# The first layer's down product in two groups of three token tiles, the contexts in the first

## The chip, the cores and the metric

The kernel runs on one core of a Trainium2 chip. The metric is the device time of one execution in microseconds (us). Three timed runs of the kernel before gave 1691.24, 1693.2 and 1694.03 us, a median of 1693.2.

The engines are named as the profile names them: PE (TensorE, matrix products; PEld is its weight load), DVE (VectorE), ACT (ScalarE), POOL (GpSimd) and SP (SyncE, which here issues nearly all transfers).

## The reference

Two layers over 512 latent tokens with a prefix of 256 context tokens, model width 1024. Layer 0 mixes tokens by attention, layer 1 by a state-space recurrence (S5). Each is followed by a gated convolutional feed-forward net of inner width 2816. What lies around the change is the end of layer 0 and the mixer of layer 1:

```
# end of layer 0, for the latents and, with their own m, for the contexts
x  = x + m[5] * rms_norm(conv_ffn(h), g_post_ffn)       # conv_ffn ends with  (silu(gate)*val) @ w_down
# layer 1
u  = modulate(rms_norm(x, g_pre_mix), m[0], m[1])       # 64 groups of 16 channels
for d in (forward, backward):
    bu  = einsum('blgc,gnc->blgn', u, bb[d])            # complex, 64 states a group
    h_c = scan(lb[d], bu of the contexts)               # h[t] = lb*h[t-1] + bu[t]
    h_l = scan(lb[d], bu of the latents, start = last h_c)
    y_l = y_l + readout(h_l, c[d])
o  = (gelu(y_l + d*u) @ w_glu_a) * sigmoid(gelu(...) @ w_glu_b)
```

Of the contexts layer 1 needs the end states of the scan alone: they are where the scan of the latents starts.

## The kernel before

Tokens lie in tiles of 128 rows: two of contexts (tiles 0 and 1, `range(NTC)`) and four of latents (`range(NTC, NT)`). Products in fp32 are made of three matmuls on operands split into a high and a low part (`mm3`, lines 145 to 147). A weight comes from memory as a raw tile of 512 KB over SP's queue, ACT makes its high part (L108) and DVE its low part (L109); five raw tiles and four split ones are kept.

**The down product** (`ffn0`, `ffn_down`) has two groups, each with its own pass over the 22 weight tiles of `w_down`: first the four latent tiles, then the two context tiles. An accumulator `dn` of one token tile has 1024 columns of PSUM; three such stand in one place (`big`), the fourth tile's in another. When a tile's sum is done, `post_start` squares it on ACT (L721), multiplies it by its gate row on DVE into a buffer `po` (L722, two buffers in turn) and makes its norm (L164 to L170). L727 adds the stream `px`; then come the statistics of layer 1's norm, its scale on POOL (L1007) and its shift on DVE (L1008). The result in `po` is sent (L1013) to `xc` (latents) or `xcc` (contexts), where tokens are laid out for the recurrence in steps of eight. A `po` buffer is free again when its transfer has landed. The rows of gates, scales and shifts (`rows`, 512 KB each, L982) are loaded for each group in its pool.

**The recurrence.** `ssm_turn` lays tokens out by channel: a copy (L1362), PE transposes `pu` (L1367), copies to `u` (L1370, L1372). `ssm_inputs` makes the inputs in units: products `pi` with a constant matrix `Pt` (512 KB, L1401), a copy `pe` (L1405), transposes `pb` (L1387) and two copies to `B` (L1392). A unit is 2 of 32 channel pairs for the latents (16 units), and 4 for the contexts (8 units, states in `Bc`). `ssm_spans` runs the recurrence inside spans of eight steps, in seven steps `k`: POOL multiplies (L1425), DVE multiplies (L1428) and adds (L1429, L1431). Latents have four blocks of channels, and so 4 x 7 steps; contexts two halves, 2 x 7. `ssm_carry` (L1440 to L1443, four DVE instructions) takes a state from span to span: three carries for a half of the contexts (`first`), seven for a pair of latent blocks (`local`). `states` then puts the carries into all steps of a block (L1562 to L1565), 8 copies `SA` for each block (L1572) set them for the readout `py` (L1586 to L1588), and ACT's GELU, transposes `pg` (L1607) and the split `gT` (L1612, L1613) feed the GLU product `glu`.

**What sets the order.** The framework orders each engine's instructions by a timeline of its own; in ties and waits it goes by the order in which the code emits them. Under the second group's loop the code takes steps of a generator `ssm_latents`, so the latents' turns and the first half of their input units are emitted between the context tiles' matmuls; the contexts' own turn, inputs, spans and carries follow in `ssm`. Buffers come from pools that are opened and closed in order: a pool opened where another was closed uses its memory, and its first writer waits for the last user there.

Of the kernel before, what the change touches and what calls it, by code (L numbers as in the profile page):

```python
# [19 lines left out]
P = 128  # L20
# [111 lines left out]
class Kernel:  # L132
# [693 lines left out]
    def ffn_up(self, l, acts, side, jobs, njobs, mods, before=None):  # L826
# [5 lines left out]
        self.hps = [self.pool(f"h{l}{i}", side) for i in range(len(acts))][::-1]  # L832
# [67 lines left out]
    def ffn_down(self, tiles, i, nhs, done, hold=False, jobs=None, ends=3, last=False):  # L900

        W, nc, ps = self.W, self.nc, self.ps
        half, h = NF // 2, self.h[i]
        pool, pn = self.hsp, h[0].shape[2]
        cols = range(0, pn, P)
        acc = [ps.tile([P, D], FT, name="dn", tag="big", bufs=3) for _ in tiles[len(tiles) // 4:]]
# [5 lines left out]
        def parts(f):  # L912
            for i in range(f, min(f + 3, NF)):
                if i not in ss:
                    s = pool.tile([P, 2, pn], FR, name="hs", tag="hs", bufs=nhs)
                    x = h[i // half][:, i % half]
# [10 lines left out]
        def together(fs, each):  # L927
            ws = [W.take(ahead=min(3, NF - f) if hold else 3) for f in fs]
            for f in fs:
                parts(f)  # L930
            for i in range(len(tiles)):
                for f, w in zip(fs, ws):
                    down(i, f, ss[f], w)
                    if i == len(tiles) - 1:
                        W.done()
                each(i)

        together(range(3), lambda i: None)
        for f in range(3, NF - ends):
# [4 lines left out]
            if jobs:  # L944
                for _ in range(17 * (f - 2) // 15 - 17 * (f - 3) // 15):
                    next(jobs, None)
        together(range(NF - ends, NF), lambda i: done(tiles[i], acc[i]))

    def ffn0(self):
# [41 lines left out]
        xcc = None  # L991
        begun = []

        def begin(t, acc, wk, rows):
            begun.append((t, self.post_start(t, acc, [rows[0], rows[0]], src, wk, 2, 2)))
# [3 lines left out]
        def end(wk, rows):  # L999
# [5 lines left out]
            _, sh, gs = rows  # L1005
# [3 lines left out]
            dst, i, parts = (xc, t - NTC, 2) if t >= NTC else (xcc, t, 4)  # L1009
            n, c = P // TC, D // parts  # L1010
            for a in range(parts):
                p0 = P // parts * a + n * i
                nc.sync.dma_start(dst[p0:p0 + n], o[:, a * c:(a + 1) * c])  # L1013

        def group(i, tiles, hold, jobs, ends, nhs):
            wk = self.pool(f"wkE{i}", "left" if i else "right")
            rows = rows_of(wk, i)
# [6 lines left out]
            self.ffn_down(tiles, i, nhs, done, hold, jobs, ends)  # L1024
            wk.release()
            self.hsp.release()
            if i == 0:
                self.wkD.release()
            self.hps[i].release()

        group(0, range(NTC, NT), False, None, 4, 5)
        sb1 = self.pool("ssmB1", "right")
        self.sb = [sb0, sb1]
        self.hsp = self.pool("hsc")
        self.W.fence = self.glu0
        self.W.limit = self.glu0 + 4
        lats = self.ssm_latents(xc)
        next(lats)
        xcc = self.xcc
        group(1, range(NTC), True, lats, 4, 4)  # L1040
        for _ in lats:
            pass
# [407 lines left out]
    def ssm_latents(self, xc):  # L1450

        nc, sb1 = self.nc, self.sb[1]
        su = self.su = self.pool("ssmu", "right")
        self.banks = (("aux", 2),)
        self.lam_tile(su.tile([P, 2048], FT, name="lam"))
        u = self.u = su.tile([P, G, NCL], FT, name="u")
        uv = u.rearrange("p (a g) j -> p g a j", a=2)
        self.xp = self.pool("ssmp", "right")
        self.xcc = self.xp.tile([4 * NCC, TC, D // 4], FT, name="xcc")
        sx = self.pool("ssmx", "right")  # L1460
        mats = self.ssm_ahead([(self.Pd, gp, 2) for gp in range(0, G // 4, 2)], ((sx, "Pt", 3),))
        next(mats)
        xqs = sb1.tile([P, 4, 8, TC, GC], FT, name="xq", tag="B", bufs=1)
        yield
        for b in range(4):
            yield from self.ssm_turn(xc[:, :, b * P:(b + 1) * P], xqs[:, b], uv[:, 8 * b:8 * b + 8], (nc.scalar, nc.scalar))
        B = self.B = [x.tile([P, 2, NCL + 1, 2, 2, 8], FT, name="B", tag="B", bufs=1) for x in self.sb]
        spans = self.spans = [self.ssm_spans(su, B[b // 2][:, b % 2:b % 2 + 1, 1:], b) for b in range(4)]
        self.us = lambda b: B[b // 2][:, b % 2, 1:], lambda g: u[:, g], NCL
        for gp in self.ssm_inputs(mats, *self.us, sx, 1, (0, G // 4)):  # L1470
            for b in range((gp + 2) // 8):
                if next(spans[b], self) is not self:
                    break
            yield
        sx.release()

    def ssm_contexts(self, mats, sc, si):

        nc, v = self.nc, self.nc.vector
        xq = si.tile([P, 16, TC, GC], FT, name="xqc")  # L1480
        uc = si.tile([P, 16, 4, NCC], FT, name="uc")
        for _ in self.ssm_turn(self.xcc, xq, uc, (v, nc.scalar, v, nc.scalar)):
            pass
        Bc = self.Bc = [sc.tile([P, 2, NCC, 2, 2, 8], FT, name=f"Bc{i}") for i in range(2)]
        self.cspans = [self.ssm_spans(sc, Bc[i], 2 * i) for i in range(2)]
        for gp in self.ssm_inputs(mats, lambda b: Bc[b // 2][:, b % 2], lambda g: uc[:, g % 16, g // 16], NCC, si, 1):
            yield gp

    def ssm(self):
        tc, nc, v = self.tc, self.nc, self.nc.vector  # L1490
        ps, W, u = self.ps, self.W, self.u
        lamR, lamI = self.lam
        sc = self.pool("ssmc")
        si = self.pool("ssmi")
        mats = self.ssm_ahead([(self.Pd, gp, 2) for gp in range(0, G // 2, 2)], ((self.wp, "raw", 5),))
        next(mats)
        W.behind, W.fence = (self.mark,), None
        W.ensure(self.glu0 + 4)
        tiles = []

        def get(ks):
            for k in ks:
                while len(tiles) <= k:
                    tiles.append(next(mats))
                yield tiles[k]

        lats = self.ssm_inputs(get(range(8, 16)), *self.us, si, 1, (G // 4, G // 2))
        self.banks = (("big", 3),)
        for gp in self.ssm_contexts(get(range(16)), sc, si):
            if gp >= 16:  # L1510
                self.banks = (("aux", 2),)
                for _ in range(2):
                    next(lats, None)
                self.banks = (("big", 3),)
        self.banks = (("aux", 2),)
        for _ in lats:
            pass
        si.release()
        self.xp.release()
        sp = self.pool("ssms")  # L1520
# [3 lines left out]
        self.banks = (("aux", 2), ("aux", 2), ("big", 3))  # L1524
        B = self.B
# [3 lines left out]
        def first(i):  # L1529

            spans = [*self.spans[2 * i:2 * i + 2], self.cspans[i]]
            while spans:
                for x in list(spans):
                    if next(x, self) is self:
                        spans.remove(x)
            x = self.Bc[i][:, :, 7]
            for s_ in range(8, NCC, 8):
                last = s_ == NCC - 8
# [255 lines left out]
```

## Time and profile before

| | kernel before |
|---|---|
| timed runs | 1691.24, 1693.2, 1694.03 us |
| profiled execution | 1692.19 us, of which the span of the trace is 1690.4 us |
| mean granted TensorE clock | 0.957 |
| PE busy | 1543.8 us (91%) |
| DVE busy | 1060.1 us (63%) |
| ACT busy | 745.8 us (44%) |
| POOL busy | 169.8 us (10%) |
| DMA | 256.03 MB, mean 151 GB/s |

The span runs from the first to the last recorded instruction, and the execution's time is 1.8 us longer. Shares are averages over the whole span; what a stage costs is read in the rows of that stage. PE's share is high in all but one long stretch, between the end of the down product and the GLU product of layer 1. Times in rows count from the span's start.

### The profile page before, as it was taken

To read this page: it belongs to the slowest core of one execution; us is meant where nothing else is said; L and a number is where in the kernel's file an instruction comes from. 1 tells how busy PE (TensorE), PEld (TensorE's weight loads), DVE (VectorE), ACT (ScalarE), POOL (GpSimd) and SP (SyncE) were. 2 spreads that over 40 slices of the span, in tenths; PEclk is the share of its full clock that TensorE was granted. 3 is DMA by queue.
4 is the path that set the end of the run, shared out by engine and by line. 5 is a ranking of instruction groups with operands and counts; after the bars stand their busy time and mean duration, and the time that the engine had idled before them with its cause. 6 is when DMAs were issued, how large, how long until landed. Compare 5 with 4: busy or idle time off the path is not lost.

```text
span 1690.4 us, 23335 instructions
## 1 busy us (share of the span) xinstructions
PE 1543.8 (91%) x8724; PEld 1228.7 (73%) x8724; DVE 1060.1 (63%) x2052; ACT 745.8 (44%) x1438; POOL 169.8 (10%) x170
## 2 busy tenths in 40 slices
PE   5999689999999999999999987725899999999997
PEld 2776469888888887778788875414678887778886
DVE  4554577768767777867643586699446655455334
ACT  4465457756434332323332356525645433333322
POOL 0111240000000000000000113366011000000000
PEclk7999799999999999999999998876899999999999
DMA  9424460087445656775853596643453234433421
GB/s 306 143 74 130 159 217 26 26 263 244 140 120 166 204 153 189 189 201 159 221 179 100 165 290 210 178 141 103 147 156 120 88 112 125 126 99 113 149 75 50
DMA packets 219847, 256.03 MB, mean 151 GB/s; under 512 B 20318, under 2 KB 171782, under 8 KB 219094
## 3 DMA queue, kind: packets, MB, share of 16 engines
q1 hardware_dynamic: 219302, 254.46, 49.2%
q8 instruction: 69, 1.13, 0.3%
q14 instruction: 44, 0.36, 0.1%
q0 software_dynamic: 384, 0.07, 0.0%
q10 hardware_dynamic: 48, 0.01, 0.0%
HBM read 216.55 MB, written 34.80 MB: 149 GB/s over the span
## 4 chain that ended last, share of the span: by engine, by line
PE 75%; DVE 11%; DMA 6%; ACT 4%; issue 2%; SPq 1%; POOL 0%; DVEq 0%; ACTq 0%; POOLq 0%
PE up L145 12%; PE up L147 11%; PE up L146 11%; PE dn L145 5%; PE dn L146 5%; PE dn L147 5%; PE acc L145 2%; PE acc L147 2%; PE acc L146 2%; PE glu L145 2%; PE glu L147 2%; PE glu L146 2%; PE macc L287 2%; DMA wm<-in_w_mod 1%; DVE t L1428 1%
## 5 line engine op out<-in xcount | busy, mean ns | idle before, releaser
L109 DVE TENSOR_TENSOR whl<-wraw,whl 128x1024 fp32r<-128x1024 f32 x202 | 250.2, 1243 | 210.9 <-ACT whl L108 207.5
L108 ACT ACTIVATE whl<-wraw 128x1024 fp32r<-128x1024 f32 x206 | 217.0, 1056 | 240.6 <-PE dn L147 141.8
L145 PE MATMUL up<-b,whl 128*128 128x256 f32 (+1 forms) x728 | 243.4, 337 | 2.6 <-DVE h L857 2.5
L147 PE MATMUL up<-b,whl 128*128 128x256 f32 (+1 forms) x728 | 241.4, 335 | 0.5 <-DVE whl L109 0.5
L146 PE MATMUL up<-b,whl 128*128 128x256 f32 (+1 forms) x728 | 241.6, 334 | 0.0
L146 PE MATMUL dn<-whl,hs 128*128 128x512 f32 x440 | 172.5, 394 | 5.0 <-DVE whl L109 5.0
L147 PE MATMUL dn<-whl,hs 128*128 128x512 f32 x440 | 171.7, 393 | 0.0
L145 PE MATMUL dn<-whl,hs 128*128 128x512 f32 x440 | 171.4, 394 | 0.0
L145 PEld LDWEIGHTS up<-b,whl 128*128 128x128 f32 x728 | 136.9, 189 | 26.4 <-issue 6.1
L146 PEld LDWEIGHTS up<-b,whl 128*128 128x128 f32 x728 | 137.3, 189 | 16.3 <-issue 2.0
L147 PEld LDWEIGHTS up<-b,whl 128*128 128x128 f32 x728 | 136.4, 189 | 16.5 <-issue 2.2
L146 PE MATMUL up<-c,whl 128*128 128x512 f32 (+1 forms) x384 | 142.6, 373 | 0.1
L147 PE MATMUL up<-c,whl 128*128 128x512 f32 (+1 forms) x384 | 141.9, 372 | 0.0
L145 PE MATMUL up<-c,whl 128*128 128x512 f32 (+1 forms) x384 | 140.8, 375 | 1.1 <-DVE c L338 1.1
L857 DVE SCALAR_TENSOR_TENSOR ga<-up,cw,ga 128x511 f32<-128x511 f32 (+1 forms) x132 | 86.8, 658 | 84.5 <-ACT ga L853 83.1
L853 ACT ACTIVATE ga<-up,cw 128x512 f32<-128x512 f32 x66 | 46.5, 705 | 151.5 <-PE up L147 149.8
L857 DVE SCALAR_TENSOR_TENSOR h<-up,cw,h 128x511 f32<-128x511 f32 (+1 forms) x132 | 86.7, 657 | 37.0 <-ACT h L853 35.9
L146 PEld LDWEIGHTS dn<-whl,hs 128*128 128x128 f32 x440 | 83.1, 189 | 24.5 <-DVE whl L109 6.7
L145 PEld LDWEIGHTS dn<-whl,hs 128*128 128x128 f32 x440 | 83.0, 189 | 18.6 <-ACT ga L853 0.4
L147 PEld LDWEIGHTS dn<-whl,hs 128*128 128x128 f32 x440 | 83.2, 189 | 18.1
L145 PEld LDWEIGHTS up<-c,whl 128*128 128x128 f32 x384 | 71.3, 188 | 18.0 <-issue 4.5
L147 PEld LDWEIGHTS up<-c,whl 128*128 128x128 f32 x384 | 72.3, 188 | 13.4 <-issue 0.4
(352 smaller groups left out, 3009.3 us busy)
## 6 DMA issues: line engine op xcount, KB each, us to landing
wraw<-in_w_up SPq DMA_DIRECT2D x88, 512.0 KB
wraw<-in_w_mod SPq DMA_DIRECT2D x80, 512.0 KB
wraw<-in_w_down SPq DMA_DIRECT2D x66, 512.0 KB
wraw<-in_w_o SPq DMA_DIRECT2D x24, 512.0 KB
Pt<-Pd SPq DMA_DIRECT2D x24, 512.0 KB
Pt<-Qd SPq DMA_DIRECT2D x32, 384.0 KB
wm<-in_w_mod SPq DMA_DIRECT2D x16, 512.0 KB
Pd<-Pb SPq DMA_DIRECT2D x16, 512.0 KB
```

What stands on the lines that cost most here:

```text
L108: nc.scalar.activation(w[:, 0], r, AF.Copy)
L109: e.tensor_tensor(w[:, 1], r, w[:, 0], op=OP.subtract)
L145: nc.tensor.matmul(out, a[0], b[0], start=start, stop=False)
L146: nc.tensor.matmul(out, a[0], b[1], start=False, stop=False)
L147: nc.tensor.matmul(out, a[1], b[0], start=False, stop=stop)
L287: nc.tensor.matmul(acc[32 * q:32 * q + 32], self.cT[:, k, :], w[:, 256 * q:256 * q + 256], start=(k == 0), stop=(k == KD - 1))
L853: nc.scalar.activation(o, acc, AF.Identity, scale=c[:, 1:2], bias=c[:, 3:4])
L857: nc.vector.scalar_tensor_tensor(x, acc[:, a + s:b + s], c[:, tap:tap + 1], x, op0=OP.mult, op1=OP.add)
L1428: v.tensor_tensor(t1, L[:, :, :, k - 1], lr[:, :, None].to_broadcast(shape), op=OP.mult)
```

## The change

The two groups of the down product become groups of three tiles. The first has both contexts and the first latent tile, the second the other three latent tiles. `ffn_down` takes `pieces`, which say from which of the two inner activations each tile's columns come. There are two sets of `rows` in the first group (latent and context), and a new one (`rows_10024` below) for the second.

The contexts no longer go straight to `xcc`: they are written to a buffer in device memory (`xnd`, L1019) and read back into `xcc` (L1486). The generator that runs under the second group's loop is now `ssm_contexts`: the contexts' turn, inputs, spans and carries, 30 steps spread over the loop's passes 6 to 17, which end with the states `C0` from which the latents start. Ahead of the last four passes a function `before` takes what is left of the generator, opens the pool of the second group's posts (`wkE1`) where the contexts' pools were, loads its rows and opens the pool of the latents' `Pt`. The latents' turns, all 16 of their input units, spans and carries are emitted behind the second group, in `ssm`. The contexts' `Pt` tiles and the latents' are loaded apart (16 + 16 loads in place of 24). The first weights of the GLU may be loaded only after the latents' inputs have been emitted (`W.limit`). The last tile's `xc` goes over ACT's queue.

In the order that comes of it, the first group's three tiles have their posts as before. Of the contexts' work, 16 `pu`, 50 of 64 `pi` and 24 of 32 `pb` matmuls stand among the second group's down matmuls, and 14 `pi` and 8 `pb` behind the last of them; the latents' 32 `pu` follow these. The fourth of the contexts' eight units has its `pb` 67 down matmuls ahead of the last one.

```diff
-        self.hps = [self.pool(f"h{l}{i}", side) for i in range(len(acts))][::-1]
+        self.hps = [self.pool(f"h{l}{i}", side) for i in range(len(acts))]
...
-    def ffn_down(self, tiles, i, nhs, done, hold=False, jobs=None, ends=3, last=False):
+    def ffn_down(self, tiles, pieces, nhs, done, jobs=None, ends=3, last=False, before=None):
...
-                    nc.scalar.activation(s[:, 0], x, AF.Copy)
-                    nc.vector.tensor_tensor(s[:, 1], x, s[:, 0], op=OP.subtract)
+                    for j, lo, hi in pieces:
+                        x, c = self.h[j][i // half][:, i % half, lo:hi], slice(o, o + hi - lo)
+                        nc.scalar.activation(s[:, 0, c], x, AF.Copy)
+                        nc.vector.tensor_tensor(s[:, 1, c], x, s[:, 0, c], op=OP.subtract)
...
-                for _ in range(17 * (f - 2) // 15 - 17 * (f - 3) // 15):
-                    next(jobs, None)
+                n, a, z = jobs[0], 6, NF - ends
+                for _ in range(n * (max(f + 1, a) - a) // (z - a) - n * (max(f, a) - a) // (z - a)):
+                    next(jobs[1], None)
+        if before:
+            before()
...
+            if t < NTC:
+                nc.sync.dma_start(self.xnd[t * P:(t + 1) * P, :], o)
+                return
+            n, c, q = P // TC, D // 2, nc.scalar if t == NT - 1 else nc.sync
...
+        wk = self.pool("wkE0", "right")
+        rows = [rows_of(wk, i) for i in range(2)]
+        tiles = range(NTC + 1)
+        self.ffn_down(tiles, ((1, 0, CTX), (0, 0, P)), 5, done_of(wk, rows, tiles), ends=4)
...
+        self.W.fence = self.W.limit = self.glu0
+        jobs = self.ssm_contexts()
...
+        def before():
+            for _ in jobs:
+                pass
+            rest["wk"] = wk = self.pool("wkE1")
+            rest["rows"] = [rows_of(wk, 0), None]
+            self.sx = self.pool("ssmx", "right")
+            self.mats = self.ssm_ahead([(self.Pd, gp, 2) for gp in range(0, G // 2, 2)],
+                                       ((self.wp, "raw", 5), (self.sx, "Pt", 3)))
+            next(self.mats)
...
+        self.ffn_down(tiles, ((0, P, LAT),), 4, done, jobs=(30, jobs), ends=4, before=before)
...
+    def ssm_contexts(self):
...
+        for a in range(4):
+            nc.sync.dma_start(xcc[NCC * a:NCC * a + NCC],
+                              dap(self.xnd, a * (D // 4), [[TC * D, NCC], [D, TC], [1, D // 4]]))
...
+        mats = self.ssm_ahead([(self.Pd, gp, 2) for gp in range(0, G // 2, 2)], ((si, "Pt", 3),))
...
+        def half(i):
+            yield from self.ssm_spans(su, Bc[i], 2 * i)
...
+                o = self.C0[:, i] if last else sc.tile([P, 2, 2, 2, 8], FT, name="cc", tag="cc", bufs=3)
+                self.ssm_carry(su, i, o, x, Bc[i][:, :, s_ + 7])
...
+        first = half(0)
+        for gp in self.ssm_inputs(mats, lambda b: Bc[b // 2][:, b % 2], lambda g: uc[:, g % 16, g // 16], NCC, si, 1):
+            if gp >= 12:
+                next(first, None)
+                next(first, None)
+            yield
+        for _ in first:
+            yield
+        yield from half(1)
+        si.release()
+        sc.release()
...
     def ssm(self):
...
+        for b in range(4):
+            for _ in self.ssm_turn(self.xc[:, :, b * P:(b + 1) * P], xq[:, b], uv[:, 8 * b:8 * b + 8],
+                                   (nc.scalar, nc.vector)):
+                pass
...
+        for gp in self.ssm_inputs(self.mats, lambda b: B[b // 2][:, b % 2, 1:], lambda g: u[:, g], NCL, self.sx, 1):
...
+        W.behind, W.fence, W.limit = (self.mark,), None, self.glu0 + 4
```

DVE at the end of the second group, before: splits of activations and weights, the gate product of the first context tile (`po`, L722), and among them copies of the latents' turn (`u`).

```order
L918 TENSOR_TENSOR hs<-h_4326,hs 128x256
L109 TENSOR_TENSOR whl_9929<-wraw_9767,whl_9929 128x1024
L918 TENSOR_TENSOR hs<-h_4326,hs 128x256
L1370 COPY u<-pu 128x4x2x64
L722 TENSOR_TENSOR po<-dn,rows_9327 128x512
L1370 COPY u<-pu 128x4x2x64
L722 TENSOR_TENSOR po<-dn,rows_9327 128x512
L723 TENSOR_TENSOR sp<-sp 128x1
```

The same place after: `cc`, `cw` and `C` belong to the contexts' carries, `Bc` to their states, and L722 is the gate product of the second group's first tile.

```order
L1466 TENSOR_TENSOR cw<-cc,lam 128x64
L1467 TENSOR_TENSOR cw<-cc,lam 128x64
L1468 TENSOR_TENSOR cw<-cw,Bc_9488 128x64
L1469 TENSOR_TENSOR C_9388<-cw 128x64
L722 TENSOR_TENSOR po<-dn,rows_10024 128x512 x2
L723 TENSOR_TENSOR sp<-sp 128x1
L722 TENSOR_TENSOR po<-dn,rows_10024 128x512
```

Between the last split of the second group's activations and its first L722, DVE now has all 66 instructions of the contexts' spans and carries (14 steps of three, six carries of four); before, these stood behind the posts of the second group.

SP before, where the second group's rows are loaded: between two early weight tiles of that group.

```order
L811 DMA wraw_9053<-in_w_down 128x1024
L982 DMA rows_9327<-md_3544 128x1024
L982 DMA rows_9327<-md_5424 128x1024 x2
L714 DMA px<-xd_3585 128x1024 x2
L811 DMA wraw_9058<-in_w_down 128x1024
```

SP after, from the last weight tile of the second group on; `Qd` holds the readout's matrices.

```order
L811 DMA wraw_9907<-in_w_down 128x1024
L1375 DMA Pt<-Pd 128x1024 x13
L1375 DMA Pt<-Qd 128x768 x8
L1375 DMA Pt<-Pd 128x1024 x6
L991 DMA rows_10024<-md_3544 128x1024
L991 DMA rows_10024<-md_5424 128x1024 x2
L714 DMA px<-xd_3585 128x1024 x2
```

The rows' load moved from the group's start behind its last weight and behind `Pt` loads. Its memory was that of `Bc`, and its wait is on the last instruction that reads `Bc`: L1468 above, three lines ahead of the L722 that needs the rows.

## Rows read from the trace of the kernel before

**Rows 1.** Windows by stage: busy of PE, PEld, DVE, ACT, POOL; clock; DMA share, GB/s.

```profile
961.00:1041.50 80.50, 72.70 (x326) 58.30 (x326) 57.65 (x91) 45.37 (x80) 11.63 (x5) 0.98 0.81 240
1041.50:1168.60 127.10, 60.96 (x465) 36.00 (x461) 108.14 (x201) 62.92 (x109) 78.96 (x77) 0.73 0.53 158
```

**Rows 2.** One tile's instructions, 840 to 1042 us: `dn`, with first and last start.

```profile
L145 PE MATMUL dn<-whl,hs x264: 388/389/628, 843.7 to 1040.4; 128*128 128x512 f32 x132
```

**Rows 3.** Timeline of PE: start us, us, what [idle before].

```profile
1037.63 0.40 PE L145 MATMUL dn<-whl,hs 128*128 128x512 f32 x1
...
1040.83 0.39 PE L147 MATMUL dn<-whl,hs 128*128 128x512 f32 x1
...
1168.56 1.97 PE L1607 MATMUL pg<-ident,yg 128*128 128x128 f32 x8 [8.48 <-ACT yg L1589]
```

**Rows 4.** Chain that ended last: start us, us, what (end of down product on).

```profile
1024.90 0.87 PE pu L1367 x8
...
1048.99 1.97 PE pi L1401 x8
1050.97 1.06 PE pb L1387 x4
...
1069.53 2.82 PE pu L1367 x12
...
1074.39 2.88 PE pi L1401 x40
```

**Rows 5.** The same chain, 945 to 1012 us, posts of the first group.

```profile
952.28 1.27 ACT junk L721 x4
...
966.00 0.61 SPq L1013
966.66 6.01 DMA xc<-po
...
989.62 0.70 DVE po L722
...
996.52 1.28 DVE po L1008
...
1002.72 4.98 DMA wraw<-in_w_down
```

**Rows 6.** Groups by line, 1041.5 to 1168.6: busy us, mean ns | idle before.

```profile
L1425 POOL TENSOR_TENSOR t<-Bc,lam 128x128 f32<-128x128 f32 x28 | 16.3, 601 | 11.2 <-DVE Bc L1431 11.2
...
L1431 DVE TENSOR_TENSOR Bc<-Bc,t 128x256 f32<-128x256 f32 x14 | 7.7, 548 | 0.8 <-POOL t L1425 0.7
...
L1428 DVE TENSOR_TENSOR t<-B,lam 128x256 f32<-128x256 f32 x28 | 20.1, 732 | 6.5 <-ACT B L1392 6.3
...
L1429 DVE TENSOR_TENSOR B<-B,t 128x256 f32<-128x256 f32 x28 | 14.1, 517 | 0.2
...
L1431 DVE TENSOR_TENSOR B<-B,t 128x256 f32<-128x256 f32 x14 | 5.9, 423 | 0.7
...
L1440 DVE TENSOR_TENSOR cw<-B,lam 128x64 f32<-128x64 f32 x8 | 1.7, 218 | 0.1
...
L1442 DVE TENSOR_TENSOR cw<-cw,B 128x64 f32<-128x64 f32 x7 | 2.5, 363 | 0.0
...
L1443 DVE TENSOR_TENSOR B<-cw 128x64 f32<-128x64 f32 x9 | 4.1, 457 | 0.1
...
L1563 DVE TENSOR_TENSOR t<-B,lam 128x1792 f32<-128x1792 f32 x2 | 5.1, 2536 | 0.0
...
L1572 ACT ACTIVATE SA<-B 64x512 f32<-64x512 f32 x16 | 16.6, 1083 | 21.0 <-DVE B L1565 20.9
```

**Rows 7.** The same chain behind the first `pg`.

```profile
1171.24 0.62 DVE gT L1613
...
1177.42 2.04 DVE t L1563
1179.55 5.62 issue
```

More of the change, by code (lines that the diff above doesn't have):

```diff
@@ L927, in together @@
         def together(fs, each):
-            ws = [W.take(ahead=min(3, NF - f) if hold else 3) for f in fs]
+            ws = [W.take(ahead=3) for f in fs]
             for f in fs:
@@ L1008, in end, with done_of @@
             self.mark = v.scalar_tensor_tensor(o, o, r, sh, op0=OP.mult, op1=OP.add).ins
[L1009 to L1017, printed above, removed]
+            if t < NTC:
+                nc.sync.dma_start(self.xnd[t * P:(t + 1) * P, :], o)
+                return
+            n, c, q = P // TC, D // 2, nc.scalar if t == NT - 1 else nc.sync
+            for a in range(2):
+                p0 = NCL * a + n * (t - NTC)
+                q.dma_start(xc[p0:p0 + n], o[:, a * c:(a + 1) * c])
+        def done_of(wk, rows, tiles):
             def done(t, acc):
@@ L1470, in ssm_latents @@
[L1470 to L1473, printed above, removed]
-            yield
[L1475 to L1485, printed above, removed]
-        for gp in self.ssm_inputs(mats, lambda b: Bc[b // 2][:, b % 2], lambda g: uc[:, g % 16, g // 16], NCC, si, 1):
-            yield gp
+        for _ in self.ssm_turn(xcc, xq, uc, (nc.scalar, nc.scalar, nc.scalar, nc.scalar)):
+            yield
@@ L1492, in ssm @@
         lamR, lamI = self.lam
[L1493 to L1497, printed above, removed]
-        W.ensure(self.glu0 + 4)
[L1499 to L1520, printed above, removed]
+        up = self.pool("ssmv")
+        u = up.tile([P, G, NCL], FT, name="u")
@@ L1529, in first @@
         def first(i):
-            spans = [*self.spans[2 * i:2 * i + 2], self.cspans[i]]
-            while spans:
-                for x in list(spans):
+            left = spans[2 * i:2 * i + 2]
+            while left:
+                for x in list(left):
                     if next(x, self) is self:
[L1535 to L1538, printed above, removed]
-                o = B[i][:, :, 0] if last else sc.tile([P, 2, 2, 2, 8], FT, name="cc", tag="cc", bufs=3)
-                self.ssm_carry(sc, i, o, x, self.Bc[i][:, :, s_ + 7])
-                x = o
+                        left.remove(x)
         def local(i):
@@ L1635, in ssm @@
         sp.release()
[L1636 to L1637 removed]
+        up.release()
+        su.release()
     def glu(self):
@@ L1735, in done @@
             nc.sync.dma_start(self.out[0, (t - NTC) * P:(t - NTC + 1) * P, :], x)
-        self.ffn_down(range(NTC, NT), 0, 5, done, ends=4, last=True)
+        self.ffn_down(range(NTC, NT), ((0, 0, LAT),), 5, done, ends=4, last=True)
         wk.release()
```

94 lines of the change are left out of this document (51 added, 43 removed).

## The prediction

> **What bounds the kernel now.** I read the windows by stage first. Up to 1041.5 us PE is busy for 72.70 of 80.50 us: the second group of the down product is a PE stage. From 1041.5 to 1168.6 us, while the recurrence is made ready, PE is busy for 60.96 of 127.10 us at a granted clock of 0.73, and DVE for 108.14 [rows 1]. This is the stretch the change is aimed at. Then I fixed its ends: the first down matmul starts at 843.7 [rows 2], the last at 1040.83, and the first transpose `pg`, from which the GLU product follows, at 1168.56 [rows 3]. So the down phase takes 197.5 us to 1041.2 and the tail behind it, from there to `pg`, 127.4. Last I read the chain of waits and the groups by line for the price of each link [rows 4 to 7]. In the tail of before the latents are turned already, so their input units start while the context tiles' posts still run, and the contexts' work is laid in between.
>
> The question is thus what stands between the last down matmul and `pg`: before, the two context tiles' posts and their work, with the latents' inputs and spans beside them; after, the three latent tiles' posts, and all the latents' work behind them. The order shows one thing more. The contexts' work isn't done when the last down matmul is, and the latents' posts stand behind it on DVE.
>
> **Term 1, the down phase.** Both kernels have 3 x 264 = 792 down matmuls [rows 2]. Fourteen start in 1040.83 - 1037.63 = 3.20 us [rows 3], 0.2286 each, so 181.0 us are the floor. 24 `up` matmuls stand among them, of half the columns, which I take at half the pace: 2.7 us. The latents' 32 `pu` cost 4 x 0.87 = 3.5 [rows 4]. What is left of 197.5 is about 10 us of stalls (7.8 of them in the second window, 80.50 - 72.70 [rows 1]). After: the 32 `pu` leave (-3.5). The contexts' 16 `pu` and 24 `pb` come in at 0.87/8 = 0.11 each, together 4.4 (a `pb` is a transpose of the same size), and 50 `pi` at 2.88/40 = 0.072 [rows 4], 3.6: +8.0. The stalls I leave as they are. The junction of the groups still has one: the third tile's L722 needs a `po` buffer, and so the landing of the first tile's transfer. The first tile's post takes 13.7 us from its first square to the issue (952.28 to 966.00) and the transfer 0.6 + 5.0 to 6.0 [rows 5], 19.3 to 20.3. The third tile's sum is ready two tiles of 24 matmuls, 11.0 us, behind the first's, and PE wants its accumulator again after 36 more, 8.2 us: 19.2. With the two gate products (2 x 0.7) behind the landing PE stands for 1.5 to 2.5 us; ACT and DVE can add some more with weight splits that they run late. Term 1 is -3.5 + 8.0 = **+4**; from -6 with all stalls gone to +14 with twice as many.
>
> **Term 2, the tail.** After, this is the chain that I expect from the last down matmul to `pg`; the running sum stands in brackets.
> - a. The contexts' last input unit. Its second `Pt` tile uses the buffer of a tile that the last but one unit frees only behind the last down matmul, so a load of 512 KB, 5.0 us [rows 5], and a unit of 1.97 + 1.06 = 3.0 [rows 4]: 8.0.
> - b. Seven span steps of the contexts' second half, which need all its inputs. Each is two POOL products at 0.601, one DVE sum at 0.548, and some 0.1 of hand-over, 1.85 [rows 6]: 13.0 (21.0).
> - c. Three carries at 2 x 0.218 + 0.363 + 0.457 = 1.25 (L1441 taken like L1440) [rows 6]: 3.8 (24.8).
> - d. The rows of gates and scales, whose memory was `Bc`'s and which may start only when the last carry has read it: the first 512 KB, 5.0 [rows 5] (29.8).
> - e. The posts of the first two latent tiles, whose sums are long there: as in before from the first square to the issue, 13.7 [rows 5] (43.5). A table load that this stretch holds stands for the one ahead of the GELU below.
> - f. Issue and landing of `xc`, which frees a `po` buffer for the third tile: 0.61 + 6.01 = 6.6 [rows 5] (50.1).
> - g. The third tile's post, 989.62 to 996.52 + 1.28 = 8.2, and its own `xc`, 6.6 [rows 5] (64.9).
> - h. The latents' turns, 2.8 for 12 `pu` at the low clock, four units at 3.0 [rows 4], and about 1 for copies: 15.9 (80.8).
> - i. Fourteen span steps of the first two blocks on DVE, 0.732 + 0.517 + 0.423 + 0.1 = 1.77 each [rows 6]: 24.8 (105.6). Further units lie beside it.
> - j. Seven carries at 1.25, and between them four steps of the third block (0.732 + 0.517 = 1.25; its third part is POOL's) [rows 6]: 13.8 (119.4).
> - k. Four instructions of `states` at 2.54 and one more such step [rows 6]: 11.4 (130.8).
> - l. Sixteen copies `SA` at 1.083, all ahead of the first GELU on ACT [rows 6]: 17.3 (148.1).
>
> 148.1 - 127.4 = **+21**. The bounds: if the contexts' work were ready at the last down matmul, a to d (29.8) would go and, with the posts then starting tile by tile, most of e: down to -20. If loads queue behind the readout's `Qd` tiles and a transfer takes 10 us as the slower of the two `xc` did, d, f and g give some 12 more: +33.
>
> On d, f and g a rule can be weighed. The 512 KB weight load took 4.98 us and the `xc` transfer 6.01 [rows 5]. The Trainium skill, "DMA: Bandwidth & Descriptors", section "Anatomy of one DMA", gives a transfer about 2.0 us fixed plus its bytes at 436 GB/s, for the software path; by it 512 KB would take about 3.2 us as an estimate and each half of `xc` 2.6. The four transfers of the chain would then be some 10 us shorter and the time about 1715. The rows above are longer than that by half and more, on this kernel's hardware queue with other transfers beside them, so I stay with the rows.
>
> **Term 3, behind the first `pg`.** Before, DVE goes from the first `gT` at 1171.24 to `states` of the third block at 1177.42, 6.2 us, and then a weight's split waits 5.62 us for issue [rows 7]. After, between its first `gT` and that point stand four steps of the fourth block (5.0), about seven and a half carries at 1.25 (9.4), a weight split (1.2) and eight `gT` at 0.62 (5.0): 20.6, so 14.4 more, of which the 5.6 of waiting can take its share: **+8**. Ends: 0, if GLU matmuls cover it, and +14.
>
> **The sum.** 4 + 21 + 8 = 33 us on the profiled execution's 1692.2: 1725.2. The median of the runs shown is 1.0 above the profiled execution: **1726 us**. Nothing behind the GLU changes, and what the change does ahead of the first down matmul (the inner activations' order) is the same work; I cost it at 0. The second group's weight splits for three tiles in place of two cost ACT and DVE nothing more: a weight is split once per group, 22 + 22 as before.
>
> **The rivals.**
>
> A, the contexts are ready in time. If the generator's steps, paced over passes 6 to 17, were not late (units at 3 us each from pass 7 on would need 24 us of some 85), the contexts' carries end some 8 us ahead of the last down matmul, the rows are loaded, and a to d leave the path. The posts of the first two tiles then lie beside down matmuls, as the four latent tiles' did in before. The tail falls to 148.1 - 50.1 = 98, and the sum is 4 - 29 + 8 = -17, so about 1676. For it: PE has the matmuls' room, and POOL is free (11.63 busy of 80.50 [rows 1]). Against it: the last 14 `pi` stand behind the last down matmul on PE, and PE goes in order. It decides if the chain a to d is over by 33 us earlier than I reckon. 5%.
>
> B, no change: the chain is shorter in several places and meets 127 us. It needs 33 us off 148, or A by half. 5%, with 1688 to 1697.
>
> C, the second group starves. It is my chain with one more mechanism: the 22 weights and 16 `Pt` of the contexts, 512 KB each, come over the queue in about half of 201 us: 38 of them are 20 MB, 200 GB/s; before, the second group's window had 240 GB/s at a DMA share of 0.81 [rows 1]. With three `Pt` buffers and the weights ahead of them on SP, a unit whose tile isn't there holds PE, and the down matmuls behind it, for 3 us as the loads above its own. Six of eight units so: +18, about 1744. For it: PE is in order, and the units stand among the down matmuls. Against it: the rate needed is under the one seen. 20%.
>
> My forecast, slower by the contexts' late end and the latents' posts behind it: 70%, 1708 to 1744.
>
> **How the numbers follow.** A measurement of this kernel tells about 0.2% (3.4 us) from no change. Faster: A, 5%. Same: most of B, 3%. Slower: C, the forecast and the rest of B, 92%. The range takes the forecast and C with their bounds, and reaches down to half of terms 1 and 3 and the short transfers: 1700 to 1756. A and B, with 10%, and some extremes are left out.
>
> **What would show it.** Right: in the trace after, DVE's first L722 of the second group starts some 30 us behind the last down matmul, released by the rows' transfer; the third tile's L722 is released by the landing of `xc`; the latents' `pu` start some 65 us behind the last down matmul, and PE is nearly idle until then, its granted clock at the low level; the first `pg` comes about 148 us behind it. Wrong: the first L722 of the second group beside the last down matmuls (A), or a down phase of 210 us and more with PE waiting for `Pt` (C). A tail under 127 us would make the prediction wrong altogether.

## The result, and the profile after

The changed kernel took 1752.83 us (median of four runs, 1750.59 to 1755.67), the kernel before 1693.62 on the same chip: a ratio of 1.0349, 95% interval 1.0324 to 1.0373. It is slower, as forecast, and by 59 us where 33 were forecast. The profiled execution has a span of 1751.9 us, 61.5 more than before.

I cut both spans at the same four points: the first down matmul, the end of the last one, the first `pg`, and the first `up` matmul of layer 1.

| stretch, us | before | after | forecast | measured |
|---|---|---|---|---|
| first to last down matmul (term 1) | 197.5 | 215.8 | +4 | +18.3 |
| from there to the first `pg` (term 2) | 127.4 | 158.7 | +21 | +31.3 |
| from there to the first `up` (term 3) | 134.5 | 146.8 | +8 | +12.3 |

The rest differs by 0.4. In such a table a term of a sum can be checked by itself. It is also steadier than the whole: ahead of the first down matmul all kernels below run nearly the same work (those with groups of three have moved 24 `up` matmuls behind it), and yet it starts between 836.2 and 847.4 us in their profiles. What causes that I didn't look into.

The ends of the stretches after, from the tile's instructions and from PE's timeline; they answer to [rows 2, 3]. The last down matmul starts at 1058.7 and ends at 1059.1:

```profile
L145 PE MATMUL dn<-whl,hs x264: 387/389/796, 843.3 to 1058.3; 128*128 128x512 f32 x132
...
L147 PE MATMUL dn<-whl,hs x264: 387/389/628, 843.9 to 1058.7; 128*128 128x512 f32 x132
```

```profile
1217.79 0.47 PE L1624 MATMUL pg<-ident,yg 128*128 128x128 f32 x1 [7.00 <-ACT yg L1606]
```

The first `up` matmul of layer 1, before and after:

```profile
L145 PE MATMUL up<-c,whl x300: 279/389/499, 1303.1 to 1500.0; 128*128 128x512 f32 x118, 128*128 128x256 f32 x32
```

```profile
L145 PE MATMUL up<-c,whl x217: 277/389/499, 1364.6 to 1499.9; 128*128 128x512 f32 x77, 128*128 128x256 f32 x32
```

The windows by stage, with columns as in [rows 1]:

```profile
930.00:960.00 30.00, 22.68 (x95) 18.35 (x94) 20.73 (x42) 12.30 (x26) 4.77 (x3) 0.92 0.30 105
980.00:1000.00 20.00, 17.71 (x75) 14.32 (x74) 5.90 (x9) 8.03 (x13) 0.00 (x0) 0.91 0.94 296
1059.10:1126.60 67.50, 3.37 (x36) 1.57 (x36) 33.94 (x80) 12.19 (x32) 15.41 (x16) 0.56 0.48 125
1172.70:1208.00 35.30, 7.14 (x54) 5.78 (x55) 34.39 (x46) 11.18 (x14) 25.13 (x16) 0.56 0.04 12
```

In the two windows of the down phase in which PE stands still its clock falls to 0.92 and 0.91. In the 67.5 us behind the last down matmul PE is busy for 3.37, DVE for half the time and no other engine for a quarter: the mark of a chain in which each link waits for the one ahead. From 1172.7 to 1208.0 DVE is busy for 34.39 of 35.30: there the path is DVE's work. DVE's timeline shows the links (idle time and what ended it in brackets):

```profile
1066.67 0.43 DVE L1454 TENSOR_TENSOR t<-Bc,lam 128x256 f32<-128x256 f32 x1 [11.59 <-ACT Bc L1418]
...
1081.29 0.23 DVE L1469 TENSOR_TENSOR C<-cw 128x64 f32<-128x64 f32 x1
1085.34 0.69 DVE L722 TENSOR_TENSOR po<-dn,rows 128x512 f32<-128x512 f32 x1 [3.82 <-DMA rows<-md]
...
1106.52 0.69 DVE L722 TENSOR_TENSOR po<-dn,rows 128x512 f32<-128x512 f32 x1 [6.68 <-DMA xc<-po]
```

DVE waits for the contexts' last inputs until 1066.67, ends their last carry at 1081.5, waits for the rows that may load only then, and after two posts for a `po` buffer. The chain of waits goes on to the latents' turn, which answers to the `xc` and `pu` links of [rows 4, 5]:

```profile
1059.73 3.33 DMA Pt<-Pd
...
1099.87 0.58 SPq L1024
1100.50 5.90 DMA xc<-po
...
1117.38 0.67 ACTq L1024
1118.09 7.88 DMA xc<-po
1126.06 0.44 DVE xq L1388
1126.63 5.35 PE pu L1393 x24
```

In the down phase PE stood still for something else twice (the view of waits: us in total, times, longest):

```profile
PE dn L145 <- DVE po L722: 7.3, 1, 7.3
PE pu L1393 <- ACT xcc L1388: 2.3, 1, 2.3
```

The first is the junction, where the third tile's accumulator comes free; the second is the contexts' turn, whose copy on ACT waited for their way through device memory. No matmul of the down phase waited for a weight or for `Pt`.

### The profile page after: what moved, and what is told of

Its sections match the earlier page's. It is cut to its first block, busy times and chain, and to the rows that moved or that the text cites. A ratio compares the mean times of both kernels' runs of the same rounds, so it can differ in the third digit from the quotient of the medians.

```text
span 1751.9 us, 23403 instructions
## 1 busy us (share of the span) xinstructions
PE 1545.5 (88%) x8724; PEld 1231.1 (70%) x8724; DVE 1065.2 (61%) x2076; ACT 749.3 (43%) x1460; POOL 169.3 (10%) x170
## 4 chain that ended last, share of the span: by engine, by line
PE 74%; DVE 11%; DMA 7%; ACT 4%; issue 2%; SPq 1%; POOL 0%; ACTq 0%; DVEq 0%; POOLq 0%
PE up L145 11%; PE up L146 10%; PE up L147 10%; PE dn L145 5%; PE dn L147 5%; PE dn L146 5%; PE acc L145 2%; PE acc L147 2%; PE acc L146 2%; PE glu L145 2%; PE glu L147 2%; PE glu L146 2%; PE macc L287 1%; PE wo L147 1%; DMA wm<-in_w_mod 1%
## 5 line engine op out<-in xcount | busy, mean ns | idle before, releaser
L146 PEld LDWEIGHTS up<-b,whl 128*128 128x128 f32 x728 | 137.9, 190 | 15.2 <-issue 1.6
```

What stands on the lines that cost most here:

```text
L146: nc.tensor.matmul(out, a[0], b[1], start=False, stop=False)
```

## The experiments

Three theories stood against each other. Theory 1: the time goes into a serial chain, the contexts' late end, the rows' load, the posts, `xc`, the latents. Theory 2: the second group is starved by the loads and matmuls added to it. Theory 3: groups of three tiles cost the time by themselves. Ratios are to the kernel before, run beside it on the same chip; differences in us are differences of ratios times 1693.6, and by the intervals such a difference is uncertain by some 5 to 7 us. Stretches are from one profile of each kernel. Pooloff and nospan3 leave the down phase as it is, and it is 0.7 and 1.9 us longer there than in the changed kernel, so a difference of some 2 us in one stretch shows nothing.

| kernel | ratio, 95% interval | down | tail | behind |
|---|---|---|---|---|
| before | 1 | 197.5 | 127.4 | 134.5 |
| changed | 1.0349 [1.0324, 1.0373] | 215.8 | 158.7 | 146.8 |
| nospan | 1.0249 [1.0219, 1.0280] | 215.6 | 146.4 | 148.0 |
| late | 1.0133 [1.0105, 1.0160] | 196.4 | 147.2 | 147.0 |
| npo3 | 1.0222 [1.0198, 1.0245] | 212.0 | 151.2 | 146.8 |
| poolturn | 1.0325 [1.0290, 1.0360] | 213.9 | 157.8 | 148.7 |
| nounit | 1.0095 [1.0061, 1.0129] | 203.6 | 130.3 | 149.8 |
| pooloff | 1.0287 [1.0257, 1.0317] | 216.5 | 155.3 | 143.2 |
| nospan3 | 1.0295 [1.0261, 1.0328] | 217.7 | 159.3 | 140.3 |
| late2 | 1.0077 [1.0051, 1.0102] | 191.3 | 137.0 | 153.7 |
| late3 | 1.0042 [1.0025, 1.0059] | 191.7 | 132.5 | 151.8 |
| b_npo3 | 0.9947 [0.9929, 0.9964] | 200.2 | 107.8 | 146.9 |
| b_pooloff | 0.9981 [0.9964, 0.9998] | 196.9 | 122.7 | 138.2 |
| b_both | 0.9912 [0.9890, 0.9934] | 197.9 | 105.3 | 143.8 |

**nospan.** Is the contexts' end on the path?

```diff
         def half(i):
-            yield from self.ssm_spans(su, Bc[i], 2 * i)
...
-                self.ssm_carry(su, i, o, x, Bc[i][:, :, s_ + 7])
...
+            v.tensor_copy(self.C0[:, i], Bc[i][:, :, NCC - 1])
```

> The changed kernel with the contexts' spans and carries left out (their end states are one copy of the last input): 66 DVE and 28 POOL instructions fewer under and behind the second group; nothing else differs. Theory 1, the serial chain behind the last down matmul: the seven steps (12.5 us in the changed kernel) and three carries (2.4 us) of the second half go, so the first L722 of the second group comes some 11 us behind the last down matmul instead of 26, and the time falls by about 15, from 1752.8 to 1738. Theory 2, the second group is starved by its added loads and matmuls: both stay, 1750 or more. Theory 3, the grouping of tiles itself costs the time: the contexts' spans don't matter, 1750 or more.

1740.19 us, some 17 less, with 12.3 of it in the tail and none in the down phase (7.1 lie ahead of the first down matmul, unexplained). The first L722 of the second group came 15.5 us behind the last down matmul (1067.29 to 1051.8), and not 11, because the rows' load, now released at 1060.8, took longer:

```profile
1060.59 0.20 DVE L1499 COPY C<-Bc 128x64 f32<-128x64 f32 x1 [27.55 <-ACT Bc L1418]
1067.29 0.69 DVE L722 TENSOR_TENSOR po<-dn,rows 128x512 f32<-128x512 f32 x1 [6.50 <-DMA rows<-md]
```

Links b and c are on the path: theory 1, against 2 and 3.

**late.** The other part of the change, undone.

```diff
-        self.ffn_down(tiles, ((0, P, LAT),), 4, done, jobs=(30, jobs), ends=4, before=before)
+        self.ffn_down(tiles, ((0, P, LAT),), 4, done, ends=4, before=before)
...
         u = up.tile([P, G, NCL], FT, name="u")
+        for _ in self.jobs:
+            pass
```

> The changed kernel with the groups of three tiles as they are, but the contexts' turn, inputs, spans and carries emitted behind the second group instead of under its loop; the second group's rows are then loaded under its loop. Theory 1, the serial chain: links a to d (26.3 us in the changed kernel) leave the path, the first two posts lie beside the last down matmuls, and the contexts' work fits beside the third post and the transfers, as in the kernel before; the down phase loses the contexts' matmuls and the stall at their copies, 10 us or more: 1705 to 1720. Theory 2, starved second group: the down phase falls by up to 18, the tail stays at 159 or grows by the contexts' work: 1735 to 1755. Theory 3, the grouping: 1745 or more.

1720.26 us: some 37 less, at the upper end of theory 1's range, but not split as it said. The down phase fell by 19.4, where 10 were named, and the tail by 11.5, where most of 26 was. The posts do lie beside the last down matmuls (first L722 at 1028.26, ahead of the last one at 1035.0). But the contexts' units, now in the tail, had their `Pt` loads there too, and PE waited for them:

```profile
PE pi L1426 <- DMA Pt<-Pd: 24.0, 11, 7.2
PE pb L1412 <- ACT pe L1430: 2.0, 3, 1.0
```

So of the 59 us some 37 (31 by the stretches) come from the contexts' work under the second group. The other 22 or more stay with groups of three, three latent posts at the end and `Pt` loaded twice; no run took these apart.

**npo3.** A third `po` buffer.

```diff
-            begun.append((t, self.post_start(t, acc, [r and r[0] for r in rows], src, wk, 2, 2)))
+            begun.append((t, self.post_start(t, acc, [r and r[0] for r in rows], src, wk, 2, 3)))
...
-                                       ((self.wp, "raw", 5), (self.sx, "Pt", 3)))
+                                       ((self.wp, "raw", 5), (self.sx, "Pt", 2)))
```

> The changed kernel with three po buffers instead of two (and two Pt buffers instead of three in the latents' own pool, to make room). Theory 1: the third tile of each group no longer waits for the landing of the first one's transfer. At the junction PE's 7.3 us of standing still falls to 2 or so, and in the tail link f (6.6 us) leaves the path with part of the third post beside the first two: 10 to 15 less, 1738 to 1743. Theory 2: the loads set the pace, 1750. Theory 3: the third post of a group of three is late because of its sum, not of the buffer: 1748 or more.

1735.43 us, some 22 less, and more than theory 1 named. In this profile 3.8 of it are in the down phase, 7.5 in the tail, and 6.9 ahead of the first down matmul, which I can't explain; only the 11.3 of the two stretches, within theory 1's 10 to 15, can be put down to the buffer. PE's wait at the junction fell from 7.3 to 1.7 us, and the third post no longer waits for a landing:

```profile
1079.36 0.69 DVE L722 TENSOR_TENSOR po<-dn,rows 128x512 f32<-128x512 f32 x1 [0.69 <-ACT junk L721]
1086.41 0.68 DVE L722 TENSOR_TENSOR po<-dn,rows 128x512 f32<-128x512 f32 x1
```

**poolturn.** The contexts' copies off ACT.

```diff
-        for _ in self.ssm_turn(xcc, xq, uc, (nc.scalar, nc.scalar, nc.scalar, nc.scalar)):
+        for _ in self.ssm_turn(xcc, xq, uc, (nc.gpsimd,) * 4):
```

> The changed kernel with the four copies of the contexts' turn on POOL instead of ACT. They wait for the contexts' way through device memory, and on ACT the weight splits of the second group stand behind them (ACT idle 8.5 us, PE 2.3 us in the changed kernel, then some matmuls at the low clock). Theory 1 with this stall as a part of the down phase's 18 us: 3 to 6 less, 1747 to 1750. If the stall is only moved to the next weight that is late (theory 2): no change, 1752 or 1753.

1753.66 us; its interval holds the changed kernel's ratio. The down phase is 1.9 shorter in one profile, and PE's wait at the turn became 2.0 us on POOL in place of 2.3 on ACT. A gain of 3 to 6 isn't shown, and with ratios that differ by 4 us it isn't ruled out either.

**nounit.** What do the contexts' matmuls cost among the down matmuls? In the changed kernel:

```profile
L147 PE MATMUL dn<-whl,hs 128*128 128x512 f32 x65 | 26.1, 405 | 0.0
...
L1427 PE MATMUL pi<-Pt,uc 128*32 128x256 f32 x100 | 9.9, 387 | 0.0
L1413 PE MATMUL pb<-ident,pe 128*128 128x128 f32 x24 | 3.6, 272 | 0.0
L1393 PE MATMUL pu<-ident,xcc 128*128 128x128 f32 x8 | 1.0, 272 | 0.0
```

```diff
-        for gp in self.ssm_inputs(mats, lambda b: Bc[b // 2][:, b % 2], lambda g: uc[:, g % 16, g // 16], NCC, si, 1):
...
+        for i in range(2):
+            nc.scalar.activation(Bc[i].rearrange("p b j r d g -> p (b j r d g)"),
+                                 x.rearrange("p a b -> p (a b)")[:, 0:2048], AF.Copy)
```

> The changed kernel with the contexts' input units left out (64 pi and 32 pb matmuls, their copies and the 16 Pt loads; the spans then work on a copy of other data), turn, spans and carries stay. The question is the down phase, 215.4 us from the first to the end of the last down matmul. In the changed kernel 100 pi, 24 pb and 8 pu records stand between 1000 and 1058.9 us, where 193 down matmuls at 0.2286 make 44.1 us: 14.8 us for them. By this count the down phase falls by 14 to 16, to about 200. By the prediction's price (50 pi at 0.072 and 24 pb at 0.11) it falls by 6.3, to 209. Theory 2, that the loads starve the second group: by more than 17. Besides, spans and carries end early, links a to d leave the tail (26 us): 1705 to 1717 in all; if the posts stay as late as they were, 1735.

1711.93 us, some 43 less. The down phase fell by 12.2 to 203.6, between the two prices and nearer to the count from the trace, though short of its 14 to 16. The tail fell by 28.4 (26 were expected), to 130.3: the first L722 of the second group starts at 1040.62, beside the last down matmul, which ends at 1041.18. So theory 1's statement on the tail holds, and the one on the down phase nearly; theory 2 wanted more than 17 there.

**pooloff.** Who lengthens link k? DVE after, and POOL beside it:

```profile
1183.03 2.58 DVE L1580 TENSOR_TENSOR t<-B,lam 128x1792 f32<-128x1792 f32 x1
1185.54 4.16 DVE L1454 TENSOR_TENSOR t<-B,lam 128x256 f32<-128x256 f32 x1
...
1198.02 5.79 DVE L1581 TENSOR_TENSOR B<-B,t 128x1792 f32<-128x1792 f32 x1
```

```profile
1183.69 5.71 POOL L1579 TENSOR_TENSOR t<-cx,lam 128x1792 f32<-128x1792 f32 x1
```

```diff
-            nc.gpsimd.tensor_tensor(t3, csf, li[:, None, 0:7].to_broadcast(shape), op=OP.mult)
+            v.tensor_tensor(t3, csf, li[:, None, 0:7].to_broadcast(shape), op=OP.mult)
```

> The changed kernel with the POOL product of states (L1579, four of 128x1792) on DVE. In the changed kernel DVE instructions that meet one of these products last 4.16 and 5.79 us in place of 0.4 and 2.0: they end when POOL's does. If DVE is held by POOL, link k (23.9 us in place of the 11.4 predicted) loses about 8 us of holding and gets 2 x 2.5 of products: 3 to 6 less in all, 1747 to 1750. If the two run side by side and DVE's long rows have another cause, each product adds its own 2.5 to the path: 1758 to 1763.

1746.16 us, 3.4 less in the tail and 3.6 behind it (3 to 6 in all were expected), though DVE has four instructions more. The same DVE rows now:

```profile
1186.35 0.41 DVE L1454 TENSOR_TENSOR t<-B,lam 128x256 f32<-128x256 f32 x1
1186.69 2.01 DVE L1579 TENSOR_TENSOR t<-cx,lam 128x1792 f32<-128x1792 f32 x1
1188.62 2.01 DVE L1581 TENSOR_TENSOR B<-B,t 128x1792 f32<-128x1792 f32 x1
```

**nospan3.** Term 3 by itself.

```diff
-        spans = [self.ssm_spans(su, B[b // 2][:, b % 2:b % 2 + 1, 1:], b) for b in range(4)]
+        spans = [self.ssm_spans(su, B[b // 2][:, b % 2:b % 2 + 1, 1:], b, 3 if b == 3 else 7) for b in range(4)]
```

> The changed kernel with the last four of the seven span steps of the latents' fourth block left out. Term 3 as predicted (a backlog of spans on DVE behind the first pg): the stretch from the first pg to the first up matmul of layer 1, 146.8 us against 134.5 in the kernel before, falls by 5 to 10, to 137 to 142, and the tail by at most 3: 1743 to 1748. If the 12 us come from the later loads of the GLU weights: unchanged, 1752.

1746.59 us; the stretch behind `pg` fell by 6.5 to 140.3, the tail didn't. So as much as half of term 3's 12.3 us hangs on these four steps on DVE.

**late2** puts late, npo3, the contexts' `Pt` in the raw buffers and the last `xc` on SP's queue together.

> A version that puts together what the runs so far point to: groups of three, the contexts' work behind the second group (late), three po buffers (npo3, with two Pt buffers for the latents), the contexts' Pt in the five raw buffers, and the last xc on SP's queue. Theory 1: late gave 36 less than the changed kernel and npo3 21; the junction's 7 us and the third post add up with late, and the 12.8 us load that the contexts' units waited for in late goes: 1690 to 1708. If the gains are the same wait taken away twice: 1715 to 1720.

1708.26 us, at the upper end of theory 1's range. The down phase, at 191.3, is shorter than before, but the last `xc` took 15.2 us beside the `Pt` loads, and the stretch behind grew to 153.7.

```profile
1043.88 12.06 DMA Pt<-Pd
1055.95 15.20 DMA xc<-po
```

**late3** has that transfer back on ACT's queue, and pooloff.

> late2 with the last xc on ACT's queue again and the products of states on DVE. In late2 this transfer took 15.2 us on SP's queue beside the Pt loads, 7.9 in the changed kernel on ACT's: 4 to 7 less if the queue made the difference, none if the engines' load did; the products give 5 to 7: 1695 to 1704 by the first, 1701 to 1704 by the second.

1702.97 us, still slower than the kernel before, and within both ranges. But the transfer itself tells them apart. Issue and first reader in late2, then in late3:

```profile
1054.98 1.53 SPq L1024 DMA_DIRECT2D xc<-po  x2
```

```profile
1071.18 2.19 ACT L1387 ACTIVATE xq<-xc 128x512 f32<-128x512 f32 x4 [3.68 <-DMA xc<-po]
```

```profile
1055.66 1.54 ACTq L1024 DMA_DIRECT2D xc<-po  x2
```

```profile
1070.90 2.20 ACT L1387 ACTIVATE xq<-xc 128x512 f32<-128x512 f32 x4 [0.90 <-DMA xc<-po]
```

From the issue to the reader 16.2 us passed on SP's queue and 15.2 on ACT's. So the queue made about 1 us of difference, and the gain of 6 in all is what the products were to give (5 to 7), as the second reading has it.

**b_npo3, b_pooloff, b_both** try in the kernel before what helped in the changed one (the edits as above, with `Pt` left at three buffers).

> The kernel before (groups of four latent and two context tiles) with three po buffers instead of two, and nothing else. In the changed kernel a third buffer gave 17 to 21 us, 3.8 of them in the down phase. Here the third and fourth latent tile wait for a landing too (DVE idle 3.4 and 2.0 us, PE 5.0 for the weight splits queued behind). If such a wait costs what stands behind it: 3 to 7 less, 1687 to 1691, all in the down phase. If the buffer matters only where the posts are the end of the chain, as in the changed kernel: no change within 2 us.

1689.15 us, 0.5% faster than before: 9 us by the ratio, where 3 to 7 were expected, and in another place: the down phase grew by 2.7, and the tail fell by 19.6. With the third post earlier, input units of the latents come to stand among the down matmuls:

```profile
1040.79 0.60 PE L1401 MATMUL pi<-Pt,u 128*64 128x256 f32 x4
1041.33 0.50 PE L147 MATMUL dn<-whl,hs 128*128 128x512 f32 x1
1041.66 0.39 PE L145 MATMUL dn<-whl,hs 128*128 128x512 f32 x1
```

Behind `pg` 12.4 us were given back.

> The kernel before with the four POOL products of states on DVE, as pooloff did with the changed kernel (6.7 us less). If DVE is held by these products wherever they run: 3 to 7 less, 1687 to 1691, half of it in the tail and half behind the first pg. If the gain belonged to the changed order alone, where DVE's backlog meets them: no change, or up to 5 more for the added DVE work.

1694.18 us, a ratio of 0.9981, whose interval ends just below 1: some 3 us, the least that was expected. The tail is 4.7 shorter and the stretch behind it 3.7 longer, and not half of the gain in each.

> The kernel before with both edits, three po buffers and the products of states on DVE. They touch different stretches (down phase; tail and behind), so the gains add: 1682 to 1688. If either doesn't hold in the kernel before: 1687 to 1694.

1682.07 us, 0.9912: faster than both kernels, and than either edit alone. By the ratios it is 15 us, and the two gains together 12: they add within the noise, though not because the edits touch different stretches: each moves the tail and what is behind it.

## Why the prediction was right, and where its sizes were off

**Direction and mechanism: right.** Nospan and nounit each take a part of the chain away and get about that part back in the tail (12.3 of 14.8 us, 28.4 where 26 were expected). Late takes links a to d away and gets 11.5 back there, since its own units then wait for `Pt`. The marks that it named are there: first L722 of the second group 26.2 us behind the last down matmul, released by the rows' transfer ("some 30"); the third tile's released by `xc`; the latents' `pu` 67.5 behind it ("some 65"), with a clock of 0.56 until then; `pg` 158.7 behind it ("about 148").

**The number was in part luck.** 1752.83 lies above the range given to the forecast itself, 1708 to 1744. It lies within the whole range only because this was widened for C, whose cause didn't occur.

**Term 1 was the worst sized, +4 against +18.3,** above its upper end of +14. The step that failed is the contexts' matmuls, "+8.0". The prediction counted 50 `pi` and took 2.88 us for 40 of them. But the trace counts 100 records for these 50 matmuls, two for each, so the 40 of [rows 4] were 20. By records it is 7.2 and not 3.6 us. Besides, a change between these small matmuls and the down matmuls costs PE some 0.1 each time: in b_npo3's rows above the next down matmul follows after 0.33 us and not 0.23, and so it does here. Together they took 14.8 + 1.6 us: from 1000 to 1058.9 us 193 down matmuls would fill 44.1 of the 58.9, and the first eight `pu` come earlier. By their own pace the small ones there are 10.7 (100 x 0.072 and 32 x 0.11); 18 such returns to the down matmuls are a part of the other 4, and the rest isn't attributed. Another 2.8 are 24 more `up` matmuls that now stand behind the first down matmul; they left the stretch ahead of it. Stalls were 10 before and are 12.9 now (215.8 - 181.0 - 5.5 - 16.4), so "the stalls I leave as they are" was nearly right, but by luck: they are others. Before, PE waited 5.0 us for weight splits and 2.8 at the latents' turn; after, 7.3 at the junction and 2.3 at the contexts' turn. The junction was forecast at 1.5 to 2.5. Its transfer was shorter than priced (2.6 us in place of 5.0 to 6.0), but the first post took 21.0 us from its first square at 931.4 to the issue at 952.39, and not 13.7, with four weight splits on DVE in between.

**Term 2, +21 against +31.3,** by its links:

| link | a | b | c | d | e | f | g | h | i | j | k | l |
|---|---|---|---|---|---|---|---|---|---|---|---|---|
| forecast | 8.0 | 13.0 | 3.8 | 5.0 | 13.7 | 6.6 | 14.8 | 15.9 | 24.8 | 13.8 | 11.4 | 17.3 |
| measured | 7.6 | 12.5 | 2.3 | 3.8 | 14.5 | 6.6 | 19.5 | 18.2 | 26.5 | 12.2 | 23.9 | 10.8 |

Eight links are within 2 us. Link g has two errors: the post took 10.9 in place of 8.2, with one DVE instruction of 3.32 us in place of 1.28 beside POOL's scale of the same tile, and its `xc`, now on ACT's queue, 8.55 in place of 6.6:

```profile
1111.44 2.34 POOL L1016 TENSOR_TENSOR po<-px,rows 128x1024 f32<-128x1024 f32 x1 [13.39 <-DVE rsx L170]
```

```profile
1111.55 3.32 DVE L1017 SCALAR_TENSOR_TENSOR po<-po,rsx,rows 128x1024 f32<-128x1024 f32 x1
```

Link k is 12.5 too long. It left out that DVE waits while POOL makes the products of `states`, 5.71 and 4.14 us: the two DVE rows shown at pooloff are 7.5 longer for it. It also counted four DVE instructions of `states` where the two blocks have six, some 3.5 more; the rest are further span steps. Half of the copies of l then lay beside k, which is why l is shorter. Pooloff shows that DVE's long rows come from POOL's products, and that only 3.4 us of the tail can be had by moving them.

**Term 3, +8 against +12.3,** within its ends. Nospan3 gives 6.5 of it to the steps named. The rest wasn't found. The stretch grows in several versions whose tail gets shorter, to 153.7 in late2, but not in all (147.0 in late), so that what leaves the tail is given back there is likely and not shown.

**The rivals.** A didn't occur: the contexts ended 22 us behind the last down matmul. Nor did B, no change. C named the right size of the down phase ("210 us and more") for a wrong cause: PE waited for no `Pt` there. The weighing of the transfers came out for the rows in the sum, 22.4 us for the four in links a, d, f and g where 23.2 were forecast, but not one by one: `Pt` and the first 512 KB of `rows` took 3.33 and 3.8 us, less than the 5.0 of [rows 5], and the second halves of `xc` 5.90 and 7.88. The Trainium skill, "DMA: Bandwidth & Descriptors", section "Anatomy of one DMA", by whose figures the estimates are 3.2 and 2.6, speaks of the software path: the trace comes near the first and not the second. Nor was it other traffic that made the first `xc` slow, as the prediction had it: while it was under way nothing else moved (last section).

## What to carry to other kernels

Filling the engines' idle time in one stage with another job didn't pay here, because the job didn't end before its host did: what was left of it, the buffers it held and the queue of one in-order engine set three transfers and two posts one behind another. Count instructions in the same view from which their price is taken. When a tail is cut, look where its work goes: in b_npo3 12.4 of 19.6 us came back behind it.

## What the runs showed of the hardware that was not expected

DVE and POOL products that take both operands from SBUF, the memory the engines share, hold each other up in these traces: a DVE product of 0.41 us lasted 4.16 when a POOL product of 5.71 was under way, and both ended within 0.3 us of each other (1189.70 and 1189.40). A DVE product that reads one operand from PSUM, where PE's sums lie, isn't held. This is the kernel before, where `dn` lies in PSUM and L722 keeps its 0.69 us inside a POOL product:

```profile
957.41 2.40 POOL L1007 TENSOR_TENSOR po<-px,rows 128x1024 f32<-128x1024 f32 x1 [110.25 <-DVE px L727]
```

```profile
958.52 0.69 DVE L722 TENSOR_TENSOR po<-dn,rows 128x512 f32<-128x512 f32 x1 [0.75 <-ACT junk L721]
```

The Trainium skill, "SBUF — State Buffer", section "Who interferes with whom", says that a DVE instruction with two SBUF inputs contends with a GpSimd instruction that reads SBUF, over a port pair that only one of them can hold at a time; these rows agree, and pooloff's do.

What a transfer takes depends on its form and on what else moves. Four stretches from a transfer's issue to its landing, with the DMA share and GB/s at their ends: `Pt` (512 KB) and the second half of `xc` (256 KB) in the changed kernel, then both in late2.

```profile
1059.73:1063.06 3.33, 1.03 (x12) 0.42 (x4) 0.00 (x0) 1.62 (x3) 0.00 (x0) 1.00 0.50 157
1100.50:1106.40 5.90, 0.00 (x0) 0.00 (x0) 0.00 (x0) 0.00 (x0) 0.00 (x0) 0.50 0.63 89
```

```profile
1043.88:1055.94 12.06, 5.07 (x30) 2.04 (x28) 7.08 (x14) 5.33 (x11) 3.27 (x3) 0.77 1.02 246
1055.95:1071.15 15.20, 7.92 (x40) 3.00 (x40) 8.91 (x19) 2.24 (x4) 7.89 (x13) 0.50 1.05 222
```

In the first two nothing else moved: 157 GB/s for 3.33 us are 512 KB, the `Pt` itself, and 89 for 5.90 are the two halves of `xc`. By itself `xc` is thus slower than `Pt`, though no larger. In late2, while 246 and 222 GB/s moved, the same transfers took 12.06 and 15.20.
